# A planner for TensorE's order: staying with the kind (fp32r or fp32) of the last instruction

## The chip, the core and the metric

The kernel runs on one core of a Trainium2 chip. The metric is the device time of one execution in microseconds (us); lower is better.

## What is computed

Two transformer layers on one sequence of 256 tokens with 1024 features, all in float32. The first has a gated linear recurrence beside a block-sparse attention of 8 heads of 128 (with 256 tokens only the own block counts), then a feed-forward part with a convolution. The second has a sliding-window attention with sinks (8 heads of 64 features, 2 key heads) beside a latent attention (8 heads, 96 features for the scores, 64 for the values), then a feed-forward part. Cut to what matters here:

```python
# second layer, both attentions
s = einsum(q, k) * scale            # window: 64 features; latent: 96
p = softmax(where(mask, s, -inf))   # window: a sink joins the sum
o = einsum(p, v)                    # 64 features a head
y = sigmoid(g_a) * (o_a @ w_o_swa) + sigmoid(g_b) * (o_b @ w_o_mla)
x = x + y @ w_out
```

The reference works in float32 throughout.

## The kernel before, in words

All activations stay in SBUF. The large products (projections, gates, feed-forward) are done in fp32r: each operand is split into a high part and the rest, and three fp32r matmuls (high by high, rest by high, high by rest) stand for one float32 product. Weights come in chunks of 1 MB or less over SyncE's queue (`produce`, from line 498); ScalarE makes the high part `wh` and VectorE the rest `wl`. On TensorE these are the rows with `wh_wp` or `wl_wp` and `r_rp`. The small products are float32: the scores of the attentions, probabilities by values, the recurrence's gates, and all transposes (a matmul with the identity `idn`, `k_cp4` in the order). One fp32 matmul that is no transpose is recorded as two.

The order on every engine is made by a planner. `_build` (line 407) calls each operation in the program's natural order; `Engines` (line 338) gives it a cost, and `Scheduler.add` (line 171) records it as an `Op` with its place `idx`, its predecessors and its tiles. `Scheduler.order` (line 207) then simulates the engines: it keeps a clock for each engine, a list of what is ready (`avail`), and for the engine that can go first it takes the ready operation with the smallest key (line 276). The key is whether it would have to wait or to load an activation table, then its place in the program. All engines' operations count in one row of 5561 places, so that a distance of 24 places is 24 operations of the whole program. `emit` (line 330) issues them in the order found; that is why nearly every instruction has line 335.

The gates of the second layer (`gate_step`) are fp32r work that fills TensorE while the attentions' softmax runs on VectorE and ScalarE. An attention of the second layer is `attend64` (line 1319): for two heads at a time the scores, the softmax, three transposes of each head's probabilities (`probs_T`, line 763), and four matmuls with the values. In the window attention the two heads' score operands lie in partitions 0 to 63 and 64 to 127 (`window_head`, line 1357), and the calls alternate between them:

```python
if window:
    for c, k in cols:
        for n in range(2):
            mm_(s[n][:, c], hs[n][0][:, (c.start > 0) * P :][:, :P], hs[n][1][:, k], start=True, stop=True)
```

Matmuls with the values write 64 partitions for one head and 64 for the other (`oo = o[64 * n : 64 * n + 64, b]`), again alternating.

The diff's functions stand here with their line numbers:

Of the kernel before, what the change touches and what calls it, by code (L numbers as in the profile page):

```python
# [10 lines left out]
F32R = mybir.dt.float32r  # L11
# [31 lines left out]
class Tile:  # L43


    def __init__(self, pool, shape, dtype, tag, name, bufs):
        self.pool, self.shape, self.dtype = pool, tuple(shape), dtype
        self.tag, self.name, self.bufs = tag, name, bufs
        self.key = (pool.name, tag)
        self.psum = pool.space is not None  # L50
        self.real = None
        self.writers, self.readers = [], []
        self.ops = 0
# [100 lines left out]


class Op:
    __slots__ = ("eng", "fn", "args", "kw", "cost", "lag", "idx", "prio", "preds", "succs", "tiles", "start", "end", "table", "left")


class Scheduler:  # L160
# [3 lines left out]
    HOP = 0.13  # L164
    SAME = {"DVE": 0.1, "ACT": 0.1}

    def __init__(self):
        self.ops = []
        self.after = ()

    def add(self, eng, fn, cost, args, kw, table=None, lag=0.0):
        op = Op()
        op.eng, op.fn, op.args, op.kw, op.cost, op.table, op.lag = eng, fn, args, kw, cost, table, lag
        op.idx = len(self.ops)
        op.prio = op.idx
        op.preds, op.succs, op.tiles = {}, [], []
        outs = [args[0]] + [kw[k] for k in ("accum_out",) if k in kw]
        ins = list(args[1:]) + [v for k, v in kw.items() if k != "accum_out"]
        span = lambda v: (0, 1 << 30) if v.tile.psum else v.span
        for v in ins:  # L180
            if isinstance(v, View):
                t, (lo, hi) = v.tile, span(v)
                for a, b, w in t.writers:
                    if a < hi and lo < b:
                        op.preds[w] = 1
                t.readers.append((lo, hi, op))
                op.tiles.append(t)
        for v in outs:
            if isinstance(v, View):
                t, (lo, hi) = v.tile, span(v)  # L190
                for lst in (t.writers, t.readers):
                    for a, b, w in lst:
                        if a < hi and lo < b and w is not op:
                            op.preds[w] = 1
                    lst[:] = [x for x in lst if not (lo <= x[0] and x[1] <= hi)]
                t.writers.append((lo, hi, op))
                op.tiles.append(t)
        for p in self.after:
            op.preds[p] = 1
        op.preds.pop(op, None)  # L200
        op.tiles = list({id(t): t for t in op.tiles}.values())
        for t in op.tiles:
            t.ops += 1
        self.ops.append(op)
        return op

    def order(self):
        ops = self.ops
        for op in ops:
            op.left = len(op.preds)  # L210
            for p in op.preds:
                p.succs.append(op)
        order_of, nxt, free = {}, {}, {}
        for op in ops:
            for t in op.tiles:
                if t not in order_of:
                    q = nxt.setdefault(t.key, [])
                    order_of[t] = len(q)
                    q.append(t)
                    free.setdefault(t.key, [0.0] * t.bufs)  # L220
        behind = {k: list(q) for k, q in nxt.items()}
        slot_at, left = {}, {t: t.ops for t in order_of}
        last_end = {t: 0.0 for t in order_of}
        waiting = {k: [] for k in nxt}
        clock = {"PE": 1.3, "ACT": 1.5, "DMA": 1.7, "DVE": 0.6}
        avail = {}
        table = [None]

        def ready(op):
            t0 = 0.0  # L230
            for p in op.preds:
                t0 = max(t0, p.end + (self.HOP if p.eng != op.eng else self.SAME.get(op.eng, 0.0)) + p.lag)
            return t0

        def blocked(t):

            f = len(free[t.key])
            return t not in behind[t.key][:f]

        def offer(op):  # L240
            for t in op.tiles:
                if t in slot_at:
                    continue
                if blocked(t):
                    waiting[t.key].append(op)
                    return
            t0 = ready(op)
            for t in op.tiles:
                t0 = max(t0, slot_at[t] if t in slot_at else min(free[t.key]) + self.HOP)
            avail.setdefault(op.eng, []).append((t0, op))  # L250

        def retry(key):
            w, waiting[key] = waiting[key], []
            for op in w:
                offer(op)

        for op in ops:
            if not op.left:
                offer(op)
        done = []  # L260
        while len(done) < len(ops):
            best = None
            for e, lst in avail.items():
                if not lst:
                    continue
                c = clock.get(e, 0.0)
                t0 = max(c, min(x[0] for x in lst))
                if best is None or t0 < best[0]:
                    best = (t0, e)
            if best is None:  # L270
                raise RuntimeError("no instruction can go next")
            t0, e = best
            lst = avail[e]
            c = clock.get(e, 0.0)

            def key(x):

                o = x[1]
                switch = o.table not in (None, "any", table[0])
                return (max(x[0], c) > t0 + 1e-9 or switch, o.prio)  # L280

            pick = min(lst, key=key)
            t0 = max(pick[0], c)
            op = pick[1]

            again = False
            for t in op.tiles:
                if t not in slot_at and blocked(t):
                    again = True
            if again:  # L290
                lst.remove(pick)
                offer(op)
                continue
            keys = []
            for t in op.tiles:
                if t not in slot_at:
                    f = min(free[t.key])
                    free[t.key].remove(f)
                    slot_at[t] = f + self.HOP
                    behind[t.key].remove(t)  # L300
                    keys.append(t.key)
                    t0 = max(t0, slot_at[t])
            lst.remove(pick)
            cost = op.cost
            if op.table not in (None, "any") and op.table != table[0]:
                table[0] = op.table
                cost += 1.28
            elif op.table == "any" and table[0] == "sqrt":
                table[0] = "exp"
                cost += 1.28  # L310
            op.start, op.end = t0, t0 + cost
            clock[e] = op.end
            done.append(op)
            for t in op.tiles:
                left[t] -= 1
                last_end[t] = max(last_end[t], op.end + op.lag)
                if left[t] == 0:
                    free[t.key].append(last_end[t])
                    keys.append(t.key)
            for k in dict.fromkeys(keys):  # L320
                retry(k)
            for s in op.succs:
                s.left -= 1
                if not s.left:
                    offer(s)
        self.time = max(op.end for op in ops)
        done.sort(key=lambda o: (o.start, o.idx))
        return done
# [66 lines left out]
def build(tc, A, out):  # L395
    from contextlib import ExitStack


    order = []
    _build(None, tc, Scheduler(), A, out, None, order)  # L400
    sch = Scheduler()
    with ExitStack() as ctx:
        _build(ctx, tc, sch, A, out, order, [])
        sch.emit(tc)


def _build(ctx, tc, sch, A, out, order, used):
    nc = tc.nc

# [1149 lines left out]
```

## Time and profile before

| | |
|---|---|
| median of 3 runs | 796.4 us (795.78 to 796.46) |
| the profiled execution's own time | 796.09 us |
| its span, first to last instruction | 794.3 us |
| TensorE busy | 783.7 us, 3879 records of 3757 instructions |
| VectorE, ScalarE busy | 571.0 us, 503.6 us |
| mean granted clock of TensorE | 0.997 |

The busy time of TensorE is a sum of overlapping records: a matmul of 512 columns has a record of 0.39 us, while the next one starts 0.23 us after it. What an instruction takes of the engine's time is read from the distance between two starts. A row of the timeline joins equal instructions that follow each other: its time is from the first one's start to the last one's end. Matmul ends are modelled.

### The profile page before, as it was taken

What the parts mean: (1) busy time and instruction counts of PE and PEld (TensorE: products, weight loads), DVE (VectorE), ACT (ScalarE), POOL (GpSimd) and SP (SyncE); (2) the same over time, 40 slices, a digit from 0 to 9 for tenths busy, and PEclk for the clock granted to TensorE, in tenths of its full rate; (3) what the DMA queues carried; (4) which work ended last, traced back from release to release, by engine and by line L of the source; (5) the groups of instructions that cost most, each with busy time, mean ns of one, the idle gap of its engine ahead of it and who ended that gap; (6) DMA issues with size and microseconds to landing.
All of it is one profiled execution on the core that took longest, in us unless ns stands there. A gap on an engine that the chain in (4) does not pass through costs nothing.

```text
span 794.3 us, 10403 instructions
## 1 busy us (share of the span) xinstructions
PE 783.7 (99%) x3879; PEld 649.5 (82%) x3879; DVE 571.0 (72%) x937; ACT 503.6 (63%) x823; POOL 5.1 (1%) x13
## 2 busy tenths in 40 slices
PE   8999999999999999999999999999999999999996
PEld 6788888888888888888888888777888888888885
DVE  5777769844665798888997675876676555459984
ACT  7979979943435776666653766777745544456552
POOL 0000000000000000000000000000000000000000
PEclk9999999999999999999999999999999999999998
DMA  8863442655645445555565444525355655554631
GB/s 291 325 233 120 160 159 106 212 187 185 211 166 185 175 167 210 166 206 177 193 242 202 160 166 159 174 93 186 118 201 162 209 168 204 167 203 161 211 107 53
DMA packets 30854, 142.53 MB, mean 179 GB/s; under 512 B 3474, under 2 KB 5268, under 8 KB 21332
## 3 DMA queue, kind: packets, MB, share of 16 engines
q1 hardware_dynamic: 29508, 138.62, 50.2%
q0 software_dynamic: 720, 2.36, 0.9%
q10 hardware_dynamic: 576, 0.89, 0.3%
q8 instruction: 30, 0.49, 0.2%
q14 instruction: 20, 0.16, 0.1%
HBM read 140.81 MB, written 1.05 MB: 179 GB/s over the span
## 4 chain that ended last, share of the span: by engine, by line
PE 95%; DMA 1%; DVE 1%; ACT 1%; SPq 0%; issue 0%; DVEq 0%
PE b_banks L335 95%; DMA wt_wp<-in_w_q 1%; DMA u_up<-in_w_k 1%; ACT t_tp L335 1%; DVE wl_wp L335 0%; SPq L335 0%; ACT wh_wp L335 0%; DVE t_tp L335 0%; DVE u_up L335 0%; ACT k_cp L335 0%; DVEq L1554 0%; DVE k_cp L335 0%
## 5 line engine op out<-in xcount | busy, mean ns | idle before, releaser
L335 PE MATMUL b_banks<-wh_wp,r_rp 128*128 128x512 f32 (+2 forms) x1520 | 477.3, 392 | 0.0
L335 DVE TENSOR_TENSOR wl_wp<-wt_wp,wh_wp 128x1024 fp32r<-128x1024 f32 (+2 forms) x182 | 297.3, 1652 | 128.5 <-ACT wh_wp L335 127.9
L335 ACT ACTIVATE wh_wp<-wt_wp 128x1024 fp32r<-128x1024 f32 (+2 forms) x182 | 250.5, 1400 | 138.2 <-PE b_banks L335 114.6
L335 PEld LDWEIGHTS b_banks<-wh_wp,r_rp 128*128 128x128 f32 x1520 | 283.1, 188 | 55.9 <-issue 1.6
L335 PE MATMUL b_banks<-wl_wp,r_rp 128*128 128x512 f32 (+2 forms) x760 | 297.3, 392 | 0.2
L335 PE MATMUL b_banks<-r_rp,wh_wp 128*128 128x512 f32 x480 | 166.8, 399 | 0.0
L335 PEld LDWEIGHTS b_banks<-wl_wp,r_rp 128*128 128x128 f32 x760 | 142.8, 188 | 29.3 <-DVE wl_wp L335 1.4
L335 PE MATMUL b_banks<-r_rp,wl_wp 128*128 128x256 f32 x480 | 125.4, 281 | 0.0
L335 PEld LDWEIGHTS b_banks<-r_rp,wh_wp 128*128 128x128 f32 x480 | 86.4, 188 | 15.7
L335 PEld LDWEIGHTS b_banks<-r_rp,wl_wp 128*128 128x128 f32 x480 | 90.3, 188 | 5.2
L335 ACT ACTIVATE t_tp<-b_banks 128x256 f32<-128x256 f32 (+2 forms) x82 | 33.8, 417 | 49.5 <-PE b_banks L335 49.3
L335 ACT ACTIVATE u_up<-b_banks,k_cp 128x512 f32<-128x512 f32 (+2 forms) x30 | 19.5, 664 | 23.9 <-PE b_banks L335 23.8
L335 ACT ACT_TABLE_LOAD x25 | 32.1, 1283 | 1.1 <-PEq L1548 0.7
L335 DVE TENSOR_TENSOR t_tp<-b_banks,t_tp 128x256 f32<-128x256 f32 (+1 forms) x76 | 26.6, 374 | 7.6 <-ACT t_tp L335 5.4
L335 ACT ACTIVATE t_tp<-b_banks,k_cp 128x256 f32<-128x256 f32 (+1 forms) x36 | 17.7, 535 | 18.9 <-PE b_banks L335 18.6
L335 DVE SCALAR_TENSOR_TENSOR t_tp<-k_cp,k_cp,t_tp 128x256 f32<-128x256 f32 x68 | 28.2, 478 | 0.0
L335 DVE TENSOR_TENSOR r_rp<-b_banks,r_rp 128x512 fp32r<-128x512 f32 x27 | 17.7, 683 | 10.9 <-ACT r_rp L335 10.6
L335 ACT ACTIVATE t_tp<-u_up 128x512 f32<-128x512 f32 (+2 forms) x22 | 13.1, 595 | 17.7 <-DVE u_up L335 17.7
L335 ACT ACTIVATE u_up<-t_tp 128x512 fp32r<-128x512 f32 x21 | 12.8, 622 | 15.7 <-DVE t_tp L335 15.7
L335 ACT ACTIVATE pr_ap<-pr_ap,s_sp 128x128 f32<-128x128 f32 (+1 forms) x48 | 21.3, 448 | 0.3
L335 ACT ACTIVATE r_rp<-b_banks 128x512 fp32r<-128x512 f32 x27 | 15.4, 592 | 7.4 <-PE b_banks L335 7.4
L335 PE MATMUL b_banks<-k_cp,t_tp 128*128 128x128 f32 (+1 forms) x112 | 16.7, 274 | 1.5 <-DVE t_tp L335 1.1
(106 smaller groups left out, 557.0 us busy)
## 6 DMA issues: line engine op xcount, KB each, us to landing
wt_wp<-in_w_gu SPq DMA_DIRECT2D x44, 512.0 KB, 4.5
wt_wp<-in_w_g SPq DMA_DIRECT2D x12, 1024.0 KB, 4.7
wt_wp<-in_w_up SPq DMA_DIRECT2D x11, 1024.0 KB, 4.8
wt_wp<-in_w_gate SPq DMA_DIRECT2D x11, 1024.0 KB, 4.8
wt_wp<-in_w_down SPq DMA_DIRECT2D x11, 1024.0 KB, 4.7
wt_wp<-in_w_down SPq DMA_DIRECT2D x22, 512.0 KB, 4.6
wt_wp<-in_w_x SPq DMA_DIRECT2D x4, 1024.0 KB, 4.8
wt_wp<-in_w_v SPq DMA_DIRECT2D x4, 1024.0 KB, 6.6
```

Of the source, the lines that this page charges most:

```text
L335: op.fn(*[get(a) for a in op.args], **{k: get(v) for k, v in op.kw.items()})
```

## The change

Each TensorE operation gets a kind: `r` where its moving operand is fp32r, `f` where it is fp32. The planner remembers the kind of the last one it put on TensorE. In the key an operation of the other kind has 24 places added where the last was `r`, and 120 where it was `f`. So a ready fp32 instruction goes ahead of ready fp32r ones only if it stands more than 24 places before them in the program, and once fp32 runs, it goes on with all ready fp32 work up to 120 places further down. The planner's clock also books 0.088 us for an `r` behind an `f`.

```diff
+    TURN, STAY = 0.088, {"r": 24, "f": 120}
...
         op.eng, op.fn, op.args, op.kw, op.cost, op.table, op.lag = eng, fn, args, kw, cost, table, lag
+        op.kind = ("r" if args[2].dtype == F32R else "f") if eng == "PE" else None
...
-        table = [None]
+        table, kind = [None], ["f"]
...
                 switch = o.table not in (None, "any", table[0])
-                return (max(x[0], c) > t0 + 1e-9 or switch, o.prio)
+                return (max(x[0], c) > t0 + 1e-9 or switch, o.prio + (self.STAY[kind[0]] if o.kind and o.kind != kind[0] else 0))
...
+            if op.kind:
+                cost += self.TURN if (op.kind, kind[0]) == ("r", "f") else 0.0
+                kind[0] = op.kind
             op.start, op.end = t0, t0 + cost
```

The instructions are the same 3757 on TensorE before and after; an fp32r instruction follows an fp32 one 120 times before and 93 times after. SyncE's and GpSimd's queues keep their order. The emitting line becomes 341.

**Place 1: TensorE in the second layer's window attention, scores of heads 2 and 3.** `b_banks194` and `b_banks195` take the scores of the two heads, `u_up83` holds the keys and `u_up81` the queries; `b_banks190` and `b_banks191` take transposes of the two heads before; `b_banks192` and `b_banks193` are a gate in fp32r. Before:

```order
L335 MATMUL b_banks191_4562<-k_cp4_247,pr_ap20_4498 128x128
L335 MATMUL b_banks193_4495<-wl_wp249_4342,r_rp46_3780 128x512
L335 MATMUL b_banks191_4562<-k_cp4_247,pr_ap20_4498 128x128 x2
L335 MATMUL b_banks194_4569<-u_up83_4197,u_up81_4248 128x128
L335 MATMUL b_banks195_4571<-u_up83_4197,u_up81_4248 128x128
L335 MATMUL b_banks194_4569<-u_up83_4197,u_up81_4248 128x256
L335 MATMUL b_banks195_4571<-u_up83_4197,u_up81_4248 128x256
L335 MATMUL b_banks192_4482<-wh_wp251_4388,r_rp47_3841 128x512 x2
L335 MATMUL b_banks187_4584<-t_tp143_4555,k_cp22_3936 64x256
L335 MATMUL b_banks187_4584<-t_tp144_4575,k_cp22_3936 64x256
L335 MATMUL b_banks187_4584<-t_tp143_4555,k_cp22_3936 64x128
L335 MATMUL b_banks187_4584<-t_tp144_4575,k_cp22_3936 64x128
```

Now, from the second score matmul of bank 194 to the first of bank 195:

```order
L341 MATMUL b_banks194_4513<-u_up83_4222,u_up81_4249 128x256
L341 MATMUL b_banks192_4483<-wh_wp248_4327,r_rp45_3777 128x512 x2
L341 MATMUL b_banks192_4483<-wl_wp249_4343,r_rp45_3777 128x512
L341 MATMUL b_banks193_4494<-wh_wp248_4327,r_rp45_3777 128x512 x2
L341 MATMUL b_banks193_4494<-wl_wp249_4343,r_rp45_3777 128x512
L341 MATMUL b_banks192_4483<-wh_wp248_4327,r_rp46_3780 128x512 x2
L341 MATMUL b_banks192_4483<-wl_wp249_4343,r_rp46_3780 128x512
L341 MATMUL b_banks193_4494<-wh_wp248_4327,r_rp46_3780 128x512 x2
L341 MATMUL b_banks193_4494<-wl_wp249_4343,r_rp46_3780 128x512
L341 MATMUL b_banks192_4483<-wh_wp248_4327,r_rp46_3780 128x512 x2
L341 MATMUL b_banks190_4548<-k_cp4_247,pr_ap19_4485 128x128
L341 MATMUL b_banks195_4553<-u_up83_4222,u_up81_4249 128x128
```

Bank 194's two score matmuls moved up by some 20 rows and stand together; bank 195's first is 11 rows behind them, between transposes of bank 190, and its second follows two transposes later.

**Place 2: TensorE a little later, scores of heads 4 to 7.** `b_banks199`, `b_banks200`, `b_banks203` and `b_banks204` take the scores of four heads, `b_banks187` the probabilities by values of heads 0 to 3. Before:

```order
L335 MATMUL b_banks187_4584<-t_tp145_4639,k_cp22_3936 64x256
L335 MATMUL b_banks187_4584<-t_tp146_4648,k_cp22_3936 64x256
L335 MATMUL b_banks187_4584<-t_tp145_4639,k_cp22_3936 64x128
L335 MATMUL b_banks187_4584<-t_tp146_4648,k_cp22_3936 64x128
L335 MATMUL b_banks193_4495<-wl_wp252_4427,r_rp48_3849 128x512
L335 MATMUL b_banks199_4661<-u_up83_4197,u_up82_4261 128x128
L335 MATMUL b_banks200_4663<-u_up83_4197,u_up82_4261 128x128
L335 MATMUL b_banks199_4661<-u_up83_4197,u_up82_4261 128x256
L335 MATMUL b_banks200_4663<-u_up83_4197,u_up82_4261 128x256
L335 MATMUL b_banks203_4672<-u_up83_4197,u_up82_4261 128x128
L335 MATMUL b_banks204_4674<-u_up83_4197,u_up82_4261 128x128
L335 MATMUL b_banks203_4672<-u_up83_4197,u_up82_4261 128x256
```

Now:

```order
L341 MATMUL b_banks191_4574<-k_cp4_247,pr_ap20_4496 128x128 x3
L341 MATMUL b_banks199_4580<-u_up83_4222,u_up82_4263 128x128
L341 MATMUL b_banks199_4580<-u_up83_4222,u_up82_4263 128x256
L341 MATMUL b_banks193_4494<-wl_wp249_4343,r_rp46_3780 128x512
L341 MATMUL b_banks192_4483<-wh_wp251_4388,r_rp47_3853 128x512 x2
L341 MATMUL b_banks192_4483<-wl_wp252_4428,r_rp47_3853 128x512
L341 MATMUL b_banks187_4596<-t_tp143_4561,k_cp22_3935 64x256
L341 MATMUL b_banks187_4596<-t_tp144_4589,k_cp22_3935 64x256
L341 MATMUL b_banks187_4596<-t_tp143_4561,k_cp22_3935 64x128
L341 MATMUL b_banks187_4596<-t_tp144_4589,k_cp22_3935 64x128
L341 MATMUL b_banks200_4604<-u_up83_4222,u_up82_4263 128x128
L341 MATMUL b_banks200_4604<-u_up83_4222,u_up82_4263 128x256
```

Where eight score matmuls of four heads stood in a row, two heads at a time in turns, bank 199's now stand before fp32r work and the group of bank 187, and bank 200's directly behind that group.

**Place 3: TensorE in the first layer, second half of the keys.** `b_banks39` and `b_banks40` take transposes of the queries `t_tp20` and `t_tp21`, `b_banks35` and `b_banks36` those of the keys; `b_banks41` is a product in fp32r. Before:

```order
L335 MATMUL b_banks38_799<-wl_wp30_752,r_rp4_188 128x512
L335 MATMUL b_banks39_882<-k_cp4_247,t_tp20_877 128x128
L335 MATMUL b_banks40_884<-k_cp4_247,t_tp20_877 128x128
L335 MATMUL b_banks39_882<-k_cp4_247,t_tp21_886 128x128
L335 MATMUL b_banks39_882<-k_cp4_247,t_tp20_877 128x128
L335 MATMUL b_banks39_882<-k_cp4_247,t_tp21_886 128x128
L335 MATMUL b_banks40_884<-k_cp4_247,t_tp21_886 128x128
L335 MATMUL b_banks40_884<-k_cp4_247,t_tp20_877 128x128
L335 MATMUL b_banks40_884<-k_cp4_247,t_tp21_886 128x128
L335 MATMUL b_banks41_904<-r_rp1_111,wh_wp32_821 128x512
L335 MATMUL b_banks41_904<-r_rp1_111,wl_wp33_833 128x256 x2
L335 MATMUL b_banks41_904<-r_rp1_111,wh_wp32_821 128x512
```

Now:

```order
L341 MATMUL b_banks39_883<-k_cp4_247,t_tp20_879 128x128
L341 MATMUL b_banks40_887<-k_cp4_247,t_tp20_879 128x128
L341 MATMUL b_banks41_889<-r_rp1_111,wh_wp32_823 128x512
L341 MATMUL b_banks41_889<-r_rp1_111,wl_wp33_835 128x256 x2
L341 MATMUL b_banks41_889<-r_rp1_111,wh_wp32_823 128x512
L341 MATMUL b_banks41_889<-r_rp2_130,wl_wp33_835 128x256
L341 MATMUL b_banks41_889<-r_rp2_130,wh_wp32_823 128x512
L341 MATMUL b_banks35_908<-k_cp4_247,t_tp18_896 128x128
L341 MATMUL b_banks36_910<-k_cp4_247,t_tp18_896 128x128
L341 MATMUL b_banks39_883<-k_cp4_247,t_tp21_892 128x128
L341 MATMUL b_banks39_883<-k_cp4_247,t_tp20_879 128x128
L341 MATMUL b_banks39_883<-k_cp4_247,t_tp21_892 128x128
```

Six fp32r matmuls stand between the first two transposes of banks 39 and 40 and the ones that need `t_tp21`, and the transposes of the keys have joined those.

## Rows read from the trace of the kernel before

**Rows 1.** The page: busy time by engine, then the chain that ended last.

```profile
PE 783.7 (99%) x3879; PEld 649.5 (82%) x3879; DVE 571.0 (72%) x937; ACT 503.6 (63%) x823; POOL 5.1 (1%) x13
...
PE 95%; DMA 1%; DVE 1%; ACT 1%; SPq 0%; issue 0%; DVEq 0%
```

**Rows 2.** Windows: stretch, length, PE, PEld, DVE, ACT, POOL busy, PEclk, DMA, GB/s.

```profile
88.90:498.40 409.50, 409.20 (x2086) 347.29 (x2084) 306.14 (x448) 258.15 (x374) 1.60 (x3) 1.00 0.51 181
498.40:559.00 60.60, 59.77 (x349) 45.53 (x349) 42.73 (x162) 46.28 (x119) 1.07 (x2) 1.00 0.45 148
559.00:787.70 228.70, 228.68 (x1044) 187.62 (x1042) 155.37 (x197) 121.04 (x164) 0.00 (x0) 1.00 0.50 168
```

**Rows 3.** Timeline of PE: start, us, operation, out<-in, array, shape, count, [idle before].

```profile
64.87 0.39 PE L335 MATMUL b_banks<-wl_wp,r_rp 128*128 128x512 f32 x1
65.10 0.27 PE L335 MATMUL b_banks<-k_cp,pr_ap 128*128 128x128 f32 x1
65.13 0.48 PE L335 MATMUL b_banks<-wh_wp,r_rp 128*128 128x512 f32 x1
65.44 0.38 PE L335 MATMUL b_banks<-k_cp,pr_ap 128*128 128x128 f32 x2
65.58 0.48 PE L335 MATMUL b_banks<-wh_wp,r_rp 128*128 128x512 f32 x1
65.89 0.39 PE L335 MATMUL b_banks<-wl_wp,r_rp 128*128 128x512 f32 x1
```

**Rows 4.** Timeline of TensorE, second attention, two small groups.

```profile
509.22 0.38 PE L335 MATMUL b_banks<-k_cp,pr_ap 128*128 128x128 f32 x2
509.53 0.93 PE L335 MATMUL b_banks<-u_up,u_up 64*128 64x128 f32 x8
510.38 0.73 PE L335 MATMUL b_banks<-wh_wp,r_rp 128*128 128x512 f32 x2
511.05 0.87 PE L335 MATMUL b_banks<-t_tp,k_cp 128*64 128x256 f32 x8
511.85 0.50 PE L335 MATMUL b_banks<-wl_wp,r_rp 128*128 128x512 f32 x1
512.18 0.62 PE L335 MATMUL b_banks<-wh_wp,r_rp 128*128 128x512 f32 x2
```

**Rows 5.** Timeline of TensorE, second attention, scores of heads 4 to 7.

```profile
518.76 1.58 PE L335 MATMUL b_banks<-u_up,u_up 64*128 64x128 f32 x16
520.27 0.73 PE L335 MATMUL b_banks<-wh_wp,r_rp 128*128 128x512 f32 x2
```

**Rows 6.** Timeline of TensorE, a group of 2 rows in the first layer.

```profile
265.03 0.28 PE L335 MATMUL b_banks<-r_rp,wl_wp 128*128 128x256 f32 x1
265.24 0.71 PE L335 MATMUL b_banks<-rows_ap,k_cp 2*128 2x128 f32 x4
265.87 0.50 PE L335 MATMUL b_banks<-r_rp,wh_wp 128*128 128x512 f32 x1
266.21 0.28 PE L335 MATMUL b_banks<-r_rp,wl_wp 128*128 128x256 f32 x1
```

**Rows 7.** Timeline of TensorE, six transposes each, alone and behind a small group.

```profile
500.70 0.86 PE L335 MATMUL b_banks<-k_cp,t_tp 128*96 128x128 f32 x6
...
504.18 0.82 PE L335 MATMUL b_banks<-k_cp,t_tp 128*96 128x128 f32 x6
```

**Rows 8.** Timeline of TensorE, transposes that wait for a copy.

```profile
87.48 0.44 PE L335 MATMUL b_banks<-k_cp,t_tp 128*128 128x128 f32 x2
88.22 0.88 PE L335 MATMUL b_banks<-k_cp,t_tp 128*128 128x128 f32 x6 [0.30 <-ACT t_tp L335]
```

**Rows 9.** Timeline of TensorE, transposes that go as their input arrives.

```profile
244.26 0.39 PE L335 MATMUL b_banks<-wh_wp,r_rp 128*128 128x512 f32 x1
244.53 0.44 PE L335 MATMUL b_banks<-k_cp,u_up 128*128 128x128 f32 x2
244.72 0.48 PE L335 MATMUL b_banks<-wh_wp,r_rp 128*128 128x512 f32 x1
```

More of the change, by code (lines that the diff above doesn't have):

```diff
@@ L156 @@
 class Op:
-    __slots__ = ("eng", "fn", "args", "kw", "cost", "lag", "idx", "prio", "preds", "succs", "tiles", "start", "end", "table", "left")
+    __slots__ = ("eng", "fn", "args", "kw", "cost", "lag", "idx", "prio", "preds", "succs", "tiles", "start", "end", "table", "left", "kind")
 class Scheduler:
```

## Prediction

> **What bounds the kernel now.** I read the page first. TensorE is busy for 783.7 of 794.3 us, and the chain of waits that ends last runs over it for 95% of the span [rows 1]. The stretches show where that is not so: from 89 us to the end of the last layer TensorE is busy for nearly all of each stretch, at a granted clock of 1.00, which is the 2.4 GHz level; 498.4 to 559 us, the second attention, lacks 0.83 us of 60.60 [rows 2]. So the kernel is worth what its 3757 TensorE instructions take one behind the other. I therefore read everything below from TensorE's timeline as distances from start to start, since records overlap and busy time hides what an instruction really costs. "Turn" is an fp32r instruction that follows an fp32 one.
>
> **What one turn costs.** In a run of fp32r matmuls of 512 columns the starts are 0.23 us apart (64.87 to 65.10). Six transposes with 0.82 us for all and 0.27 us for one are (0.82 - 0.27) / 5 = 0.11 us apart [rows 3, 7]. Now the two mixed. A transpose starts at 65.10, the fp32r matmul only 0.03 us later, and the next instruction 0.31 us after that [rows 3]. The fp32r matmul looks 0.08 us dearer than 0.23, but its predecessor shows 0.03 and not 0.11: the two together take 0.34 us, which is 0.11 + 0.23. The next group says the same: two transposes and one matmul from 65.44 to 65.89 are 0.45 us, against 0.22 + 0.23 [rows 3]. A turn between full-size instructions thus costs 0.00 to 0.01 us. The 0.088 us that the change books for one in its planner is the first half of this reading only.
>
> **What a change of the array's shape costs.** The score matmuls of the sliding-window heads use 64 rows of the array and the probability times value matmuls of the second attention use 64 columns; both come in pairs, one head in each half. The eight records at 509.53 (four of 128 columns, four of 256) take 0.85 us to the next start [rows 4]. At 0.11 and 0.22 us each, one behind the other, they would take 1.32; as pairs side by side 0.66. So they do run in pairs, and 0.19 us is added. The transposes before them take 0.31 for 0.22 (+0.09), and behind them two fp32r matmuls take 0.67 for 0.46 (+0.21, in which the next group's entry lies); the 64-column group takes 0.80 and its follower 0.33 for 0.23 (+0.10) [rows 4]. Sixteen records in one group take 1.51 us, 1.32 as pairs plus the same 0.19 [rows 5]. A group with nothing to pair with shows the price too: four records of 128 columns with 2 rows take 0.63 for 0.44 (+0.19), the fp32r of 256 columns before them 0.21 for 0.12, half of 0.23 (+0.09), the one after them 0.34 for 0.23 (+0.11) [rows 6]. One visit to a smaller shape costs about 0.39 us, paired or not. Where transposes follow it, not fp32r, six of them take 0.86 for 0.82 [rows 7]: 0.04 in place of 0.11, so 0.32 in all.
>
> **The change, part by part.** The DMA queues keep their order; ScalarE and VectorE follow TensorE's order, and what that does is in the two terms on waits.
> - *Turns.* Counted in the two orders, 120 become 93. 27 x 0.005 = -0.1 us (ends 0 and -0.3).
> - *Pairs.* Before, the scores of banks 194 and 195 stand alternately, those of 199 and 200 too. After, bank 194's second stands 11 rows ahead of 195's first, and 195's two are parted by two transposes, and 199's stand ahead of 187's group, 200's behind it. Nothing is left to run beside them: 1.32 - 0.66 = 0.66 us each, +1.3 us. Nothing covers this, since TensorE is the bound there [rows 2].
> - *Shape groups.* Banks 188 to 220 have 11 groups of 64-row or 64-column instructions before and 15 after. Before: ten leave into fp32r and one into transposes, 10 x 0.39 + 0.32 = 4.2. After: seven leave into fp32r, seven into transposes or full-size scores, and one (187) straight into 200's, which spares it about half: 7 x 0.39 + 7 x 0.32 + 0.2 = 5.2. That is +0.9 us, rounded down (ends +0.4, if a group between transposes costs half, and +1.6).
> - *Waits that go.* At 87.48 two transposes of bank 39 and 40 start, and the next only at 88.22, 0.74 - 0.22 = 0.5 us late, waiting for ScalarE's copy [rows 8]. After, six fp32r matmuls stand in this hole. Smaller ones of 0.1 us stand where a transpose goes the moment VectorE is done: 244.26 to 244.53 and 244.53 to 244.72 are 0.27 and 0.19 for 0.23 and 0.14 [rows 9]. Four places like this (this one is the pattern) get one to four fp32r ahead. -0.5 - 4 x 0.08 = -0.8 us (ends -0.4 and -1.2).
> - *Waits that come.* The denser fp32 runs ask ScalarE and VectorE for their inputs at other times, and the trace of before has no such place. From below the price is 0: VectorE has its order of the softmax steps moved along. From above I take three holes like that at 88 us, 1.4 us. I take +0.6, six small waits of 0.1, since most of the fp32 work is held back and not pulled ahead.
>
> The sum is -0.1 + 1.3 + 0.9 - 0.8 + 0.6 = +1.9 us. The profiled execution took 796.1 us (span 794.3 and 1.8 around it); the median of the three runs is 0.3 above it, so I forecast 796.4 + 1.9 = **798.3 us**. With all ends one way and the other it is +0.2 to +3.9.
>
> The Trainium skill speaks to the third term: TensorEngine Tiling (Array Packing), section Key Properties, says that a change of tiling mode drains TensorE, while separate tiles execute in parallel. The trace agrees on both: 0.85 us for eight records that would take 1.32 in a row, and some 0.39 us per visit. By that rule every switch costs alike, whatever comes next.
>
> **The rivals.**
> 1. *A turn costs what it looks like.* If the fp32r after fp32 is really 0.09 us dearer, and the 0.03 us before it an effect of the modelled starts, 27 turns give 2.4 us: +1.9 + 0.1 - 2.4 = -0.4, 796.0 us, no change. It decides from about 0.02 us a turn, where the sum falls under 1.6. For it speaks the 0.31 us; against it every span over a whole run, as 65.10 to 65.44. Chance 0.10.
> 2. *The waits go and none come.* The held-back transposes always find their inputs, and the last term is 0, the fourth at its end: -0.1 + 1.3 + 0.9 - 1.2 = +0.9, 797.3 us. For it speaks that ScalarE is busy for 63% and VectorE for 72% [rows 1]. Chance 0.22.
> 3. *Dense fp32 runs starve.* After the change several heads' transposes and scores stand together, and every head's chain (scores, maximum, exponential, sum, scaling, transposes) is followed at once by the next. If five of the sixteen heads of the second attention cost a wait of 0.5 us, as at 88 us, the sum is +1.9 - 0.6 + 2.5 = +3.8, 800.2 us. Against it: these stretches still have fp32r work from the gates between them. Chance 0.10.
> 4. *Every visit costs the whole price.* A transpose behind a group is no cheaper than fp32r, and the straight step from 187's group to 200's is as dear as any: 15 x 0.39 - 11 x 0.39 = +1.6 in place of +0.9, so +2.6, 799.0 us. Against it: the 0.86 of [rows 7]. Chance 0.13.
>
> It is the drain rule of that page of the Trainium skill, taken as it stands, that rival 4 prices.
>
> **How the numbers follow.** A difference of 0.2%, 1.6 us, is about what a measurement of this kernel can tell from none. My forecast has 0.45; two thirds of it lie above +1.6 and one third below. Slower: 0.30 of the forecast, 0.10 of rival 3 and 0.13 of rival 4, 0.53. Within 0.2%: 0.15 of the forecast, 0.20 of rival 2 and 0.07 of rival 1, 0.42. Faster: 0.02 of rival 2 and 0.03 of rival 1, where a dear turn and vanished waits meet, 0.05. The range takes in rivals 1, 2, 4 and the bounds of the forecast but its last ends: 796.0 to 800.0 us; rival 3 lies at its edge.
>
> **What would show it.** Right: in the second attention TensorE's stretch grows by some 2 us with as many instructions; four scores with 64 rows of one bank stand alone for about 0.85 us from first start to the next, as long as eight did; the number of 64-row rows in the timeline grows; the hole at 88 us is gone; the remaining turns still show 0.03 and 0.31. Wrong: if the split scores take half of that; if an fp32r run with fewer turns is shorter by 0.09 us for each; if idle rows of over 0.3 us with VectorE or ScalarE as their end stand before transposes in 500 to 560 us; or if the gain lies in a stretch with no fp32 work, which none of this explains.

## The result, and the profile after

The changed kernel takes **800.35 us** (median of 4 runs, 800.01 to 800.71) against 796.09 us for the kernel before on the same chip (4 runs): 4.3 us slower, ratio 1.0055, 95% interval 1.0043 to 1.0067. The forecast was slower, 798.3 us, range 796.0 to 800.0. The direction held, the size did not: 1.9 us were forecast, and the time lies 0.35 us above the range. The profiled execution took 800.54 us, with a span of 798.8 us.

The page of the changed kernel, busy time by engine and the chain that ended last:

```profile
PE 787.8 (99%) x3879; PEld 653.0 (82%) x3879; DVE 572.0 (72%) x937; ACT 503.8 (63%) x823; POOL 5.2 (1%) x13
...
PE 92%; ACT 4%; DMA 2%; DVE 2%; issue 0%; DVEq 0%; SPq 0%; ACTq 0%
```

As many instructions, as much work on VectorE and ScalarE [rows 1], and 4.1 us more busy time on TensorE, which also counts what a matmul waits for once it has been issued. The chain now leaves TensorE for 8% of the span, where it was 5%. The same three stretches, cut at places that answer to those of [rows 2]:

```profile
91.00:499.80 408.80, 408.34 (x2072) 345.93 (x2070) 304.56 (x445) 256.43 (x372) 1.60 (x3) 1.00 0.50 179
499.80:562.00 62.20, 60.67 (x340) 45.19 (x341) 44.10 (x163) 48.08 (x122) 1.16 (x2) 1.00 0.38 129
562.00:792.10 230.10, 230.10 (x1052) 189.68 (x1050) 155.06 (x196) 119.59 (x161) 0.00 (x0) 1.00 0.52 171
```

The granted clock is the same 1.00. The second attention has 1.53 us without TensorE where it had 0.83, and fewer records in a longer stretch.

**Where the 4.3 us are.** For each record of TensorE I took the distance to the next start, less what that kind takes unhindered in the rows: 0.227 us for 512 columns of fp32r, 0.117 for 256 and 0.173 for 384, 0.109 for a transpose, 0.109 and 0.216 for a record of an fp32 matmul with 128 and 256 columns, half of that for a matmul on 64 rows or columns. Summed, this is the engine's **surplus**: waits, visits to small shapes, and pairs that are not side by side. It comes from one profiled execution of each kernel, and 0.1 us either way depends on where a cut falls.

| stretch, by place in the program | before | after | difference |
|---|---|---|---|
| 55 us to the hole at 88 us | 0.3 | 0.9 | +0.6 |
| the hole at 88 us, to 100 us | 0.8 | 0.3 | -0.5 |
| 100 to 135 us (recurrence, first attention) | 0.5 | 1.5 | +1.0 |
| 135 us to the second attention | 3.4 | 3.6 | +0.3 |
| the second attention | 6.1 | 9.6 | +3.4 |
| behind it | 0.7 | 0.3 | -0.4 |
| sum from 55 us | 11.8 | 16.1 | +4.4 |

The first 55 us are left out: TensorE waits there for loads, and the surplus of this part differs by up to 2 us between the profiles, either way.

**What came as forecast: split pairs.** TensorE's timeline of the changed kernel, second attention, banks 194, 195, 199, 200 and the values of bank 187:

```profile
507.04 0.92 PE L341 MATMUL b_banks<-u_up,u_up 64*128 64x128 f32 x4
507.89 0.73 PE L341 MATMUL b_banks<-wh_wp,r_rp 128*128 128x512 f32 x2
...
511.41 0.49 PE L341 MATMUL b_banks<-u_up,u_up 64*128 64x128 f32 x2
511.82 0.44 PE L341 MATMUL b_banks<-k_cp,pr_ap 128*128 128x128 f32 x2
512.19 0.70 PE L341 MATMUL b_banks<-u_up,u_up 64*128 64x256 f32 x2
512.82 0.50 PE L341 MATMUL b_banks<-wl_wp,r_rp 128*128 128x512 f32 x1
...
514.06 0.92 PE L341 MATMUL b_banks<-u_up,u_up 64*128 64x128 f32 x4
514.91 0.50 PE L341 MATMUL b_banks<-wl_wp,r_rp 128*128 128x512 f32 x1
```

Four records of one head take 0.85 us to the next start (507.04 to 507.89, 514.06 to 514.91), as long as eight of two heads did [rows 4]. Bank 195, parted by two transposes, pays for two visits.

**What came as forecast: the hole at 88 us is gone.** The place of [rows 8]:

```profile
88.13 0.44 PE L341 MATMUL b_banks<-k_cp,t_tp 128*128 128x128 f32 x2
88.32 0.48 PE L341 MATMUL b_banks<-r_rp,wh_wp 128*128 128x512 f32 x1
...
89.46 1.69 PE L341 MATMUL b_banks<-k_cp,t_tp 128*128 128x128 f32 x14
```

**What was not in the forecast: new waits.** First in the second attention, at the last transposes of the latent attention's queries and keys (banks 185 and 186); behind them one row of ScalarE's timeline:

```profile
503.73 0.40 PE L341 MATMUL b_banks<-k_cp,t_tp 128*96 128x128 f32 x2 [0.70 <-DVE t_tp L341]
...
505.12 0.40 PE L341 MATMUL b_banks<-wl_wp,r_rp 128*128 128x512 f32 x1
506.28 0.83 PE L341 MATMUL b_banks<-k_cp,t_tp 128*96 128x128 f32 x6 [0.76 <-DVE t_tp L341]
```

```profile
501.88 0.47 ACT L341 ACTIVATE t_tp<-b_banks,k_cp 128x256 f32<-128x256 f32 x1 [1.97 <-PE b_banks L341]
```

505.12 to 506.28 is 1.16 us for an instruction of 0.23: a wait of 0.9 us that was not there before (504.18 [rows 7], six transposes directly behind fp32r). The wait at 503.73 is not new: the kernel before has it at 502.33, and one of 0.5 us ahead of it.

```profile
498.47 0.40 PE L335 MATMUL b_banks<-k_cp,t_tp 128*96 128x128 f32 x2 [0.37 <-DVE t_tp L335]
502.33 0.40 PE L335 MATMUL b_banks<-k_cp,t_tp 128*96 128x128 f32 x2 [0.77 <-DVE t_tp L335]
```

The scores of heads 0 and 1 now go ahead of the fp32r products that ScalarE's copy at 501.88 waits for; so the chain from copy to VectorE to transposes starts late, and the six fp32r matmuls that TensorE has meanwhile do not cover it.

Then in the first layer. The probabilities times values of its attention, before, and the same group after:

```profile
114.03 0.40 PE L335 MATMUL b_banks<-r_rp,wh_wp 128*128 128x512 f32 x1
114.27 0.28 PE L335 MATMUL b_banks<-r_rp,wl_wp 128*128 128x256 f32 x1
114.39 1.47 PE L335 MATMUL b_banks<-ptS_ap,u_up 128*128 128x256 f32 x8
```

```profile
113.28 0.48 PE L341 MATMUL b_banks<-r_rp,wl_wp 128*128 128x256 f32 x2
113.60 0.40 PE L341 MATMUL b_banks<-r_rp,wh_wp 128*128 128x512 f32 x1
113.84 0.28 PE L341 MATMUL b_banks<-r_rp,wl_wp 128*128 128x256 f32 x1
113.95 0.39 PE L341 MATMUL b_banks<-r_rp,wh_wp 128*128 128x512 f32 x1
114.38 1.57 PE L341 MATMUL b_banks<-ptS_ap,u_up 128*128 128x256 f32 x8
```

After, the fp32r matmul at 113.95 is followed 0.43 us later, 0.20 more than it takes, and the group itself takes 0.10 us longer. No idle row marks this: I read it as a matmul that was issued and stood. Between the last transposes and the products there are five fp32r matmuls, 3 x 0.117 + 2 x 0.227 = 0.81 us, where before there were seven, 1.15 us, counted in the two orders. This work is the products' **cover**: TensorE does it while the copy of the probabilities that they need is made. Three more groups like this (56, 124 and 128 us) and a wait of 0.4 us at 72 us make up most of the rest of the first layer's loss.

### The profile page after: what moved, and what is told of

It reads as the page before. It is cut to its first block, busy times and chain, and to the rows that moved or that the text cites. A ratio compares the mean times of both kernels' runs of the same rounds, so it can differ in the third digit from the quotient of the medians.

```text
span 798.8 us, 10401 instructions
## 1 busy us (share of the span) xinstructions
PE 787.8 (99%) x3879; PEld 653.0 (82%) x3879; DVE 572.0 (72%) x937; ACT 503.8 (63%) x823; POOL 5.2 (1%) x13
## 4 chain that ended last, share of the span: by engine, by line
PE 92%; ACT 4%; DMA 2%; DVE 2%; issue 0%; DVEq 0%; SPq 0%; ACTq 0%
PE b_banks L341 92%; ACT t_tp L341 1%; ACT wh_wp L341 1%; DMA wt_wp<-in_w_q 1%; DMA u_up<-in_x 1%; DVE wl_wp L341 1%; DVE t_tp L341 1%; DMA u_up<-in_w_k 1%; ACT L341 0%; ACT pr_ap L341 0%; DVE u_up L341 0%; ACT r_rp L341 0%; ACT ptS_ap L341 0%; DVE pr_ap L341 0%; ACT u_up L341 0%
## 5 line engine op out<-in xcount | busy, mean ns | idle before, releaser
L341 PE MATMUL b_banks<-u_up,u_up 128*128 128x128 f32 (+5 forms) x96 | 18.6, 338 | 0.0
```

The lines of the kernel that those rows point to most:

```text
L341: op.fn(*[get(a) for a in op.args], **{k: get(v) for k, v in op.kw.items()})
```

## Experiments

All are compared with the kernel before in runs on the same chip; "surplus" is the sum from 55 us on as above, against 11.8.

| run | time, us | against before, us | ratio, 95% | surplus against before |
|---|---|---|---|---|
| the change | 800.35 | +4.3 | 1.0043 to 1.0067 | +4.4 |
| turn0 | 798.53 | +2.8 | 1.0022 to 1.0048 | +2.4 |
| first_layer | 797.36 | +1.6 | 1.0011 to 1.0029 | +1.2 |
| second_attention | 798.97 | +3.2 | 1.0030 to 1.0055 | +3.0 |
| paired_turn0 | 796.74 | +1.0 | 1.0007 to 1.0025 | +0.3 |
| turn_only | 799.31 | +3.5 | 1.0034 to 1.0059 | +3.4 |
| split_only | 795.87 | +0.1 | 0.9991 to 1.0009 | -0.1 |
| held_scores | 796.55 | +0.8 | 1.0002 to 1.0020 | 0.0 |
| first_turn0 | 795.45 | -0.3 | 0.9988 to 1.0006 | -0.3 |
| cover_first | 795.36 | -0.7 | 0.9983 to 1.0001 | -0.7 |
| cover_pairs | 794.75 | -1.3 | 0.9975 to 0.9992 | -0.9 |
| cover_only | 796.12 | +0.4 | 0.9995 to 1.0014 | +0.4 |

**The booked turn taken out (turn0).**

```diff
-    TURN, STAY = 0.088, {"r": 24, "f": 120}
+    TURN, STAY = 0.0, {"r": 24, "f": 120}
```

> The change with TURN = 0 and the two stays as they are (TensorE: 94 turns, 15 groups of small shapes). Theory: part of the new waits comes from the 0.088 us that the planner books for a turn and that TensorE does not take, so that it counts ScalarE's and VectorE's work as done too early. Without it the fp32 products at 72, 114, 124 and 128 us get back as much fp32r work ahead of them as before, and their waits (0.1 to 0.6 us each, some 1.6 us in all) go: 798.0 to 798.8 us. The wait of 0.9 us at 505 us stays, since the order there is the same. Rival: the waits come from the stays alone; then 800.0 to 800.6 us.

+2.8 us where the change cost +4.3, in the range given for the theory. From 100 to 135 us the surplus is 0.54, that of before. The group of products:

```profile
113.92 0.28 PE L341 MATMUL b_banks<-r_rp,wl_wp 128*128 128x256 f32 x1
114.04 1.47 PE L341 MATMUL b_banks<-ptS_ap,u_up 128*128 128x256 f32 x8
```

0.12 us from start to start, and 1.47 us as before. Counted in the traces, the groups at 56, 114, 124 and 128 us have 4, 7, 3 and 11 fp32r matmuls as cover in the kernel before, 3, 5, 2 and 8 after the change, and 4, 7, 3 and 11 again here. The wait at 505 us is still there (0.8 us). But the hole at 88 us is back:

```profile
86.93 0.44 PE L341 MATMUL b_banks<-k_cp,t_tp 128*128 128x128 f32 x2
87.85 0.88 PE L341 MATMUL b_banks<-k_cp,t_tp 128*128 128x128 f32 x6 [0.49 <-ACT t_tp L341]
```

So what filled the hole in the changed kernel was not the sorting by kind alone. In turn_only below, which does not sort, the hole is gone.

**The first layer alone, the second attention alone (first_layer, second_attention).** The conditions on the kinds and on TURN hold only below place 3500, as here, or only from there (`3500 <= o.idx < 99999`):

```diff
-                return (max(x[0], c) > t0 + 1e-9 or switch, o.prio + (self.STAY[kind[0]] if o.kind and o.kind != kind[0] else 0))
+                return (max(x[0], c) > t0 + 1e-9 or switch, o.prio + (self.STAY[kind[0]] if o.kind and o.kind != kind[0] and 0 <= o.idx < 3500 else 0))
...
-                cost += self.TURN if (op.kind, kind[0]) == ("r", "f") else 0.0
+                cost += self.TURN if (op.kind, kind[0]) == ("r", "f") and 0 <= op.idx < 3500 else 0.0
```

> The change for the operations below place 3500 of the program only (all before the second attention's last transposes of queries and keys); behind it the planner works as before. Theory: this part brings the waits of the first layer and loses the hole at 88 us, and splits no pair of score matmuls: +0.6 to +1.2 us on the kernel before, 796.7 to 797.3 us. Rival (what I forecast): the first layer only gains, -0.5 to -0.8 us, 795.3 to 795.6 us, and all of the loss is in the second attention.

> The change for the operations from place 3500 on only. Theory: split pairs (+1.3), small shapes (+0.4 to +1.2) and the wait of 0.9 us at 505 us are here and need nothing of the first layer: +2.8 to +3.5 us, 798.9 to 799.6 us. Rival: the order of the second attention hurts only because the first layer shifted weights and copies; then under +2 us, below 798.1 us.

+1.6 and +3.2 us. The first is above the range given for the theory; my forecast, a gain there, falls. The second is in its range: the second attention hurts by itself. Together they give 4.8, against 4.3.

**Whole pairs (paired_turn0).** In `attend64` each score matmul of a pair holds both heads' banks, and TURN is 0:

```diff
-    TURN, STAY = 0.088, {"r": 24, "f": 120}
+    TURN, STAY = 0.0, {"r": 24, "f": 120}
...
                         mm_(s[n][:, c], hs[n][0][:, (c.start > 0) * P :][:, :P], hs[n][1][:, k], start=True, stop=True)
+                for op in sch.ops[-4:]:
+                    for t in (s[0].tile, s[1].tile):
+                        if t not in op.tiles:
+                            op.tiles.append(t)
+                            t.ops += 1
```

> The change with TURN = 0, and the four score matmuls of two window heads hold both heads' banks, so that they become free to go together (TensorE: 91 turns, 12 groups of small shapes, all pairs whole). Theory: against TURN = 0 alone it gives back 1.3 us less what was not split there, 0.6 to 1.3 us, and two visits to a small shape: 796.5 to 797.5 us, and what is left above the kernel before is the wait of 0.9 us at 505 us. Rival: a split costs half as much as I worked out, since the second head's matmuls fill other time: less than 0.5 us below TURN = 0.

1.8 us below TURN = 0 alone, and the surplus of the second attention falls from 8.8 to 6.8: the split of pairs and the extra visits that go with it cost 2.0 us there. TensorE has 91 turns here where the kernel before has 120, and no gain of that size shows: a turn costs next to nothing, as read from [rows 3].

**The booked turn alone (turn_only).**

```diff
-    TURN, STAY = 0.088, {"r": 24, "f": 120}
+    TURN, STAY = 0.088, {"r": 0, "f": 0}
```

> The change with both stays at 0: only the 0.088 us that the planner books for each turn is left, and it orders by place as before (TensorE: 124 turns, 12 groups of small shapes; one score matmul of the first pair is parted from its three). Theory: a turn that is booked and not taken makes the planner believe in covers that are not there. Products of the first layer have 0.1 to 0.2 us less fp32r work ahead of them, and only 0.68 us instead of 1.59 us of it stands between the transposes of banks 185 and 186 that wait for VectorE: +1.2 to +2.0 us on the kernel before of the same call. Rival: the stays do the harm and the booked turn does nothing: less than +0.5 us, the price of the parted score matmul.

+3.5 us, far more than expected of it: **one constant in the planner's clock, with no sorting at all, costs most of what the whole change costs.** The largest wait is the one foreseen, before banks 185 and 186:

```profile
502.73 0.70 PE L341 MATMUL b_banks<-u_up,u_up 64*128 64x256 f32 x2
504.49 0.40 PE L341 MATMUL b_banks<-k_cp,t_tp 128*96 128x128 f32 x2 [1.06 <-DVE t_tp L341]
```

The rest is small and in many places: the products of the first layer as in the changed kernel (surplus of 1.4 from 100 to 135 us), a wait of 0.4 us at 73 us, and four of 0.17 us ahead of transposes between 630 and 700 us, one in each of four steps of the last feed-forward part, where my expectation had none.

**Pairs one head behind the other (split_only).** In the kernel before:

```diff
-                for c, k in cols:
-                    for n in range(2):
+                for n in range(2):
+                    for c, k in cols:
```

> The kernel before, with the loops over columns and heads of the window scores exchanged: each head's two score matmuls stand together, the second head's directly behind, in all four pairs; nothing else is edited (123 turns, 11 groups of small shapes). Theory: two matmuls run side by side only where they stand in turns. Then a pair takes up to 1.32 us instead of 0.66 us without the visit: +2.6 us over four pairs if nothing overlaps, +1.7 us if the second head's first matmul (0.22 us) still runs beside the first head's second. Rival: TensorE runs any two matmuls in different halves side by side as long as they stand in the same group: +0.0 to +0.5 us, and a split costs only where other work stands between.

The rival holds: +0.1 us. TensorE's timeline of this run:

```profile
498.45 0.93 PE L335 MATMUL b_banks<-u_up,u_up 64*128 64x128 f32 x8
499.31 0.86 PE L335 MATMUL b_banks<-k_cp,t_tp 128*96 128x128 f32 x6
...
517.38 1.68 PE L335 MATMUL b_banks<-u_up,u_up 64*128 64x128 f32 x16
518.99 0.73 PE L335 MATMUL b_banks<-wh_wp,r_rp 128*128 128x512 f32 x2
```

Eight records take 0.86 us, sixteen 1.61 (1.51 in turns, [rows 5]). Matmuls in the two halves overlap as long as they stand in one group; they need not alternate. What the change lost is that the group was torn.

**The scores held back (held_scores).** On top of whole pairs and TURN = 0:

```diff
-                return (max(x[0], c) > t0 + 1e-9 or switch, o.prio + (self.STAY[kind[0]] if o.kind and o.kind != kind[0] else 0))
+                return (max(x[0], c) > t0 + 1e-9 or switch, o.prio + (self.STAY[kind[0]] if o.kind and (o.kind != kind[0] or 3610 <= o.idx < 3680) else 0))
```

> TURN = 0, whole pairs, and in addition the operations of places 3610 to 3679 (scores of heads 0 to 3 among them) get the stay added even behind fp32, so that the scores of heads 0 and 1 do not go ahead of the fp32r products on which the keys and queries of the latent attention hang (TensorE: 96 turns, 13 groups of small shapes, one of the groups with values in two pieces). Theory: the wait of 0.8 us before the six transposes of banks 185 and 186 goes, since the order there is that of before: 0.4 to 0.8 us less than with whole pairs and TURN = 0, so +0.2 to +0.6 us on the kernel before of the same call. Rival: that wait only moves to the next transposes, and it stays at +1.0 us.

The wait before the six transposes is gone from the timeline, as the theory says, but the time falls by only 0.2 us, less than expected, and the intervals of the two runs overlap: by the time alone this is not decided. In the surplus, the second attention falls from 6.8 to 6.5; 0.8 went, and one group with values, now in two pieces, took 0.45 of it back.

**The stays of the first layer without the booked turn (first_turn0).** The edit of first_layer with TURN = 0.

> The two stays for operations below place 3500 and TURN = 0: the first layer sorted by kind, with no booked turn (TensorE: 110 turns, 11 groups of small shapes, all pairs whole, the second attention as before). Theory: sorting by kind by itself is worth nothing, since a turn costs nothing, and harms nothing here, since the cover ahead of the products is that of before: -0.4 to +0.3 us on the kernel before of the same call. Rival: the stays of the first layer cost by themselves: +0.6 us or more, a good part of the +1.6 us that the first layer cost with the booked turn.

-0.3 us, not to be told from zero, where the same stays with TURN = 0.088 cost +1.6. A later group of products, in first_layer and then here:

```profile
128.68 0.28 PE L341 MATMUL b_banks<-r_rp,wl_wp 128*128 128x256 f32 x1
129.09 0.92 PE L341 MATMUL b_banks<-ptS_ap,u_up 128*128 128x256 f32 x4
```

```profile
127.64 0.40 PE L341 MATMUL b_banks<-r_rp,wh_wp 128*128 128x512 f32 x1
127.88 0.82 PE L341 MATMUL b_banks<-ptS_ap,u_up 128*128 128x256 f32 x4
```

0.41 us from an instruction of 0.12, against 0.24 from one of 0.23.

**The sign reversed.** If a booked turn acts by making the planner's TensorE later than the real one, a negative one should make it earlier and add cover:

```diff
-    TURN, STAY = 0.088, {"r": 24, "f": 120}
+    TURN, STAY = -0.06, {"r": 24, "f": 120}
```

with the stays below place 3500 only (cover_first); then -0.08 with the stays everywhere and whole pairs (cover_pairs); then -0.1 with both stays at 0 (cover_only).

> The two stays for operations below place 3500, and TURN = -0.06: the planner books less than a turn's own time, so that it believes TensorE to be earlier than it is by its costs and places more fp32r work ahead of what waits for ScalarE and VectorE (TensorE: 115 turns, 11 groups of small shapes, the second attention as before). Theory: the booked turn acts through cover alone, so its sign decides: with +0.088 the first layer cost +1.6 us, with 0 it cost -0.3; with -0.06 the covers ahead of the products stay those of TURN = 0 and the transposes get a little more: -0.2 to -0.9 us on the kernel before of the same call. Rival: any departure from the true cost of a turn, up or down, costs: +0.5 us or more.

> The stays everywhere, whole pairs, TURN = -0.08 (TensorE: 98 turns, 12 groups of small shapes). Theory: against whole pairs with TURN = 0, which cost +1.0 us on the kernel before, the waits ahead of the transposes of the latent attention's queries and keys (0.86 and 0.80 us there) shrink, as more fp32r work stands ahead of them: 0.5 to 1.2 us less, -0.3 to +0.5 us on the kernel before of the same call. Rival: these waits have nothing to do with the booked time, since there is no turn inside the chains of VectorE, and it stays at +1.0 us or more.

> TURN = -0.1 and both stays at 0, pairs left as they fall: no sorting by kind, only the sign of the booked turn is reversed against the run with TURN = 0.088 alone, which cost +3.5 us (TensorE: 115 turns, 13 groups of small shapes; the pair of heads 2 and 3 is parted, two of its four score matmuls stand alone). Theory: the cover does the work, not the sorting. The waits that TURN = 0.088 brought do not come, and some 0.5 us of those of the kernel before go; the parted pair and its two visits cost 0.7 to 1.0 us: between -0.2 and +0.7 us on the kernel before of the same call, 3 us or more below TURN = 0.088 alone. Rival: what the last run won came from the sorting; then without the stays this is at +1.0 us or more.

-0.7, -1.3 and +0.4 us. The first is in the range given, though its interval just takes in no change. **The second is faster than both kernels of this study** (ratio 0.9983, 0.9975 to 0.9992), by more than expected: it lies 2.3 us below paired_turn0, where 0.5 to 1.2 were given. In surplus it is 1.2; most of the rest is the end of the program, where paired_turn0 is slow (last section). How much of its gain over the kernel before the stays have, no run takes apart. The third lies 3.2 us below the run with TURN = 0.088 alone, with one pair torn; neither sorts, so between these two the sign of the booked turn decides. Transposes of the queries and keys in the second run:

```profile
496.99 0.33 PE L341 MATMUL b_banks<-wl_wp,r_rp 128*128 128x384 f32 x1
497.16 0.38 PE L341 MATMUL b_banks<-k_cp,t_tp 128*96 128x128 f32 x2
...
500.98 0.40 PE L341 MATMUL b_banks<-k_cp,t_tp 128*96 128x128 f32 x2 [0.72 <-DVE t_tp L341]
...
503.47 0.83 PE L341 MATMUL b_banks<-k_cp,t_tp 128*96 128x128 f32 x6 [0.47 <-DVE t_tp L341]
```

The first pair of transposes starts 0.17 us behind an fp32r matmul of 0.17: the wait of 0.5 us there, in the kernel before too, is gone. The other two are those that the expectation named, and they remain: 0.9 us as in paired_turn0, and 0.6 us where it was 0.8. So the gain came in part at another wait than expected.

## Why the prediction was wrong, point by point

- **What bounds the kernel: right.** VectorE and ScalarE did the same work [rows 1]; the loss is in the distances between TensorE's starts, +4.4 us.
- **Turns: right.** Runs with 91 and 110 turns are no faster than 120 for it, and a turn that is left still shows its 0.03 us and then 0.31 to 0.32 (518.24, 518.27, 518.59 us in the trace of the changed kernel). Rival 1 falls.
- **Pairs and shape groups, +1.3 and +0.9: right in sum.** Taking the new waits (0.9 us at 505 and 0.1 us at 526) off the second attention's +3.4 leaves 2.4, against 2.2; between turn0 and paired_turn0 it is 2.0. The two were not told apart by a run. That they stood alternately, on which the text laid weight, does not matter (split_only). The rule of the Trainium skill, TensorEngine Tiling (Array Packing), Key Properties, that different tiles can run in parallel, agrees with it: 0.86 us for two heads one behind the other, 0.85 alternately.
- **Waits that go, -0.8: right in size, in part by luck.** The hole at 88 us is worth -0.5, and behind the attention -0.4 went. But first_turn0 has the hole again with its stays in place, and turn_only has none: it is the booked turn that fills it, not the sorting. And of five waits of 0.1 us like that at 244 us in the trace of before (244, 256, 441, 592, 604 us) only the first is gone; most of the -0.4 is one wait of 0.25 us at 730 us, which the text did not name.
- **Waits that come, +0.6, with ends 0 and 1.4: this is the step that failed.** They are 2.9 us: 0.6, 1.0 and 0.3 in the three stretches ahead of the second attention that grew, and 1.0 in it. That is 2.3 us more than was taken, and the forecast lay 2.4 us short. The reading under it was wrong: "the trace of before has no such place" passes over the waits at 498.47 and 502.33, 0.5 and 0.9 us by the distances between starts, ahead of transposes in the second attention itself. "Most of the fp32 work is held back and not pulled ahead" was the reason for a low value, and it left out the other half of the diff. I read the 0.088 us off as no real cost, and then gave it no further thought: but the planner puts work ahead of a transpose or a product until its clock says that the input is there. A cost that it books and TensorE does not take shortens that real cover, by 0.1 to 0.6 us at the four groups counted above. The first three parts, 1.9 us, come from it: with TURN = 0 these stretches stand at 0.3, 0.5 and 3.1 us of surplus, no more than in the kernel before. The wait of 0.9 us at 505 us does not: it stays with TURN = 0 (0.8 us) and goes where the scores are held back, so it comes from the order that the stays make. Without any sorting, a change of this constant from 0.088 to -0.1 moves the kernel from +3.5 to +0.4 us (turn_only, cover_only); within the change, taking it out gives back 1.5 us.
- **Rival 3** named 800.2 us, close to the result, but by five heads' softmax chains that starve. One such wait came (0.76 us of idle time with VectorE at its end), but at the chain of queries and keys, and the rest is small waits of 0.1 to 0.4 us in the first layer. It was not that mechanism. The sign that the text had named, an idle row of over 0.3 us with VectorE at its end between 500 and 560 us, could not tell: the kernel before has such a row at 502.33. Rival 2, in which no waits come, falls with them. Rival 4 is not told apart by a run's time, but its condition does not hold in the trace of the changed kernel: two transposes between two groups (511.82 to 512.19) take 0.37 us for 0.22, 0.15 more, where fp32r in that place pays 0.21 [rows 4]; not every change of shape costs alike.
- **The range** took in the bounds of a term that was bounded by its pattern (three holes), not by what the second constant of the diff could do.

Not settled in full: why TURN = 0.088 alone costs more (+3.5) than it adds to the stays (+1.5). Part of it is the end of the program, where turn0 loses 0.6 us (last section). In surplus it is 3.4 against 2.0 us. Of the 1.4 us between them 0.7 lie behind the second attention, where turn_only has its four waits of 0.17 us, and 0.3 each in the second attention and between 55 us and the hole. Why these waits are not there with the stays, no run shows.

## What to carry to other kernels

A planner's cost constant is part of the schedule: booked time that the engine did not take removed real cover ahead of what waits, so price its effect on the order, not only whether it is true. Errors on the two sides were not alike here: 0.088 us too much a turn cost 3.5 us by itself, 0.06 to 0.1 us too little cost at most 0.4 in three runs. And sorting instructions by kind needs two prices from the trace first: that of a change of kind (here none) and that of what the sorting tears apart (here matmuls on half arrays: 0.85 us for one head alone, as long as two heads take together).

## What the runs showed of the hardware

- fp32 matmuls on 64 rows, one head in each half, overlap without alternating: sixteen records in 1.61 us, where one behind the other they would take 2.6 by an estimate (twice the 1.32 of the prediction's working).
- Lost time on TensorE, waits among it, can stand with no idle row: the engine's busy time grew by 4.1 us with the same instructions. Distances between starts show it (113.95 to 114.38 us, 0.43 for 0.23).
- Three runs (turn0, paired_turn0, held_scores) end 0.6 to 0.7 us later behind their last matmul than the ten other kernels of the study, 7.6 to 7.7 us instead of 7.0. The instructions there are the same; the last two output transfers take longer to land, 2.7 to 2.8 us (median) against 2.3 to 2.4 in the ten others. In the trace of before and of paired_turn0:

```profile
out_dram<-u_up SPq DMA_DIRECT2D x2, 128.0 KB, 2.3
```

```profile
out_dram<-u_up SPq DMA_DIRECT2D x2, 128.0 KB, 2.8
```

This is where their times lie further above the kernel before than their surplus does. What makes these transfers slower was not tried.
